# The opening stage of a decoder trunk: sums of squares, the first modulation columns and the rope angles computed on other engines

## The chip, the cores and the metric

The kernel runs on one core of one Trainium2 chip. The core has TensorE (PE: matmuls, with a separate record for each load of a stationary operand, PEld), VectorE (DVE), ScalarE (ACT), GpSimd (POOL) and SyncE (SP, which here only issues DMAs). The metric is the time of one execution on the device in microseconds (us), as the median of the runs shown.

## The reference

One layer of a decoder trunk over 512 tokens of 1024 features: a mixer of three branches (RWKV-7, forgetting attention, latent attention), then a squared-ReLU MLP, each behind a normalisation that is scaled and shifted by values computed from a vector `c`. The part that the change touches is this:

```python
c_act = jax.nn.silu(c)
mod = c_act @ w_mod[l] + b_mod[l]
sh_m, sc_m, g_m, sh_f, sc_f, g_f = [m[:, None, :] for m in jnp.split(mod, 6, axis=-1)]
h = rms_norm(x, norm_mix_pre[l]) * (1 + sc_m) + sh_m
z = h @ w_in[l]
```

and, for the rotary embedding of the latent attention:

```python
ang = positions.astype(jnp.float32)[..., None] * inv_freq
cos, sin = jnp.cos(ang), jnp.sin(ang)
```

`w_mod` is 1024 x 6144, `w_in` 1024 x 5572. Everything is float32; large products are made as three matmuls of a high and a low part (fp32r).

## The kernel before

x lies transposed: features on partitions, in 8 blocks of 128 features by 512 tokens. Scale and shift are then one number per partition: `A` and `B`, columns `d` of `self.mod[0]` and `self.mod[1]`. Block d of h is `x[d] * A * bc + B`, where `bc` holds each token's reciprocal root mean square on all partitions. `startup` (L370) does the following, in an order that is written by hand for TensorE, VectorE, ScalarE and GpSimd; SP's queue issues in program order too.

- **Loads.** `c` (one row), `cols` (small vectors as columns), the positions, four pieces of x on SP's queue, then for each block the two columns' weights `wm` (2 x 512 KB, three buffers) and the block's 896 columns of `w_in`, `raw` (448 KB, three buffers).
- **Warm-up.** `heat(n)` (L388) issues n matmuls of 128 columns on zeros, whose result isn't used. `WARM` gives the counts at five places.
- **Conditioning** (L200). `c` is broadcast to all partitions by a matmul with a row of ones, ScalarE takes tanh, VectorE forms `crow` = 2 silu(c) on all partitions, in two halves.
- **Sums of squares** (L398 to L414). ScalarE squares each block of x. VectorE adds five of them into `ssum[0]`, GpSimd three (blocks 2, 3, 4) into `ssum[1]`; TensorE sums over the partitions with 8 matmuls of one column. `rstd` and `spread` make a diagonal matrix of it, and a matmul with ones (L437) gives `bc`.
- **The block loop** (L440). For block d, `wm_load` issues the load of `wm` and computes the scale column: a product of 128 x 1024 with `crow` with its sum over the row (`mod_col`, L219), then `A` (L428). The shift column is made the same way on VectorE for block 0, and for the others by GpSimd (the product, L222) and ScalarE (the sum, L223, and the bias, L460). ScalarE rounds `raw` to `whi` (L454); VectorE makes `t` (L461), ScalarE `hi` (L462), VectorE `wlo` (L463) and `lo` (L464); then TensorE adds 21 matmuls of 512 columns to seven accumulators `zps` (L472).
- **Rope angles** (L266). A generator whose four parts are called in blocks 3 to 6 of that loop; the first three are VectorE's range reduction, the last two sines on ScalarE (with a load of their table).

Behind the loop `attn_inputs` (L479) reads `zps` and goes on with the rest of the mixer; only TensorE's order is by hand there.

Of the kernel before, what the change touches and what calls it, by code (L numbers as in the profile page):

```python
# [12 lines left out]
F32 = mybir.dt.float32  # L13
# [5 lines left out]
ALU = mybir.AluOpType  # L19
# [30 lines left out]
OUT_CUTS = (0, 384, 768, 1024)  # L50
LAST_CUTS = (0, 512, 768, 1024)
HC = 16
WARM = (1, 12, 0, 8, 4)
SUM_POOL = (2, 3, 4)
MOD0_DVE = (0,)
ROPE_D = (3, 4, 5, 6)
MM3 = 0.64
GATE_A = 7
FILL_G = 1.7
# [10 lines left out]
def _layout(fields):  # L70
# [11 lines left out]
    ("qg", 3), ("kvg", 2), ("bf", 4), ("cmul", 5), ("cadd", 5), ("invf", 32),  # L82
))
CST, NCST = _layout((
    ("bones", 128), ("dinc", 128), ("dexc", 128), ("cmask", 128),
# [13 lines left out]
class Builder:  # L99
# [99 lines left out]

    def conditioning(self, pool, pz, c):  # L200
        nc = self.nc
        th = pool.tile([P, D], F32, name="th")
        ps = [pz.tile([P, S], F32, tag="z", name="cps") for i in range(2)]
        for i in range(2):
            nc.tensor.matmul(ps[i], self.ones[0:1, :], c[:, i * S:(i + 1) * S], start=True, stop=True)
        for i in range(2):
            sl = slice(i * S, (i + 1) * S)
            nc.scalar.activation(th[:, sl], ps[i], AF.Tanh, scale=0.5)
            yield
            nc.vector.scalar_tensor_tensor(self.crow[:, sl], th[:, sl], 1.0, ps[i], ALU.add, ALU.mult)  # L210

    def pair(self, tag, name):
        return self.yp.tile([P, 2 * S], F32, tag=tag, name=name, bufs=3 if tag == "y" else 4)
# [3 lines left out]

    def mod_col(self, dst, w, cols=slice(0, D)):
        self.nc.vector.scalar_tensor_tensor(w, w, 0.5, self.crow[:, cols], ALU.mult, ALU.mult, accum_out=dst)  # L219

    def mod_col_pool(self, dst, w):
        self.nc.gpsimd.tensor_tensor(w, w, self.crow, ALU.mult)  # L222
        self.nc.scalar.activation(w, w, AF.Copy, scale=0.5, accum_out=dst)  # L223

    def mod_stream(self):
        for n, (i, d) in enumerate((i, d) for i in (2, 3, 4) for d in range(NB)):
# [143 lines left out]
    def startup(self, pz, pm):  # L370
        nc, tc, a = self.nc, self.tc, self.a
        E = mybir.EngineType
        with tc.tile_pool(name="sp", bufs=1, side="right") as sp, \
                tc.manual_schedule(engines={E.PE, E.DVE, E.Activation, E.Pool}):
            c = sp.tile([1, D], F32, name="c")
            nc.sync.dma_start(c, a["crow"])
            nc.scalar.dma_start(self.cols, a["cols"])
            self.pos = sp.tile([P, NT], I32, name="pos")
            nc.scalar.dma_start(self.pos, a["pos"])
            xt = [sp.tile([P, 2, S], F32, name=f"xt{i}") for i in range(4)]  # L380
            for i in range(4):
# [4 lines left out]
            nc.gpsimd.memset(warm, 0.0)  # L386

            def heat(n, ps=bc):  # L388
                for _ in range(n):
                    nc.tensor.matmul(ps[:, 0:P], self.ones, warm[:, 0:P], start=True, stop=True)  # L390

            heat(WARM[0])
            b1 = self.sml("b1", NB)
            rope = self.rope_tables(sp)
            cond = self.conditioning(sp, pz, c)
            next(cond, None)
            ssum = [sp.tile([P, S], F32, name=f"ssum{i}") for i in range(2)]
            for d in range(NB):  # L398
                own = d in SUM_POOL
                begin = d in (0, SUM_POOL[0])  # L400
                sq = ssum[own] if begin else sp.tile([P, S], F32, tag="sq", name="sq", bufs=4)
                nc.scalar.activation(sq, x[d], AF.Square)
                if d in (1, 3):
                    next(cond, None)
                if not begin:
                    (nc.gpsimd if own else nc.vector).tensor_tensor(ssum[own], ssum[own], sq, ALU.add)
            nc.vector.tensor_scalar(b1, self.col("b0", 0, NB), 1.0, None, ALU.add)
            heat(WARM[1])
            sums = pz.tile([P, S], F32, tag="z", name="sums")
            for i in (1, 0):  # L410
                for t in range(NT):
                    nc.tensor.matmul(sums[:, t:t + 1], ssum[i][:, t * P:(t + 1) * P], self.ones[:, 0:1],
                                     start=i == 1 and t == 0, stop=i == 0 and t == NT - 1)
                    heat(WARM[2])  # L414
            wms, accs = [], []

            def wm_load():
                d = len(wms)
                wm = sp.tile([P, 2, D], F32, tag="wm", name="wm", bufs=3)
                if d < 2:  # L420
                    nc.sync.dma_start(wm[:, 0, :], a["wmod"][:, d, 0, :])
                    nc.sync.dma_start(wm[:, 1, :], a["wmod"][:, d, 1, :])
                else:
                    nc.sync.dma_start(wm, a["wmod"][:, d, 0:2, :])
                acc = [self.sml(f"acc{i}") for i in range(2)]
                self.mod_col(acc[0], wm[:, 0, :])
                A = self.mod[0][:, d:d + 1]
                nc.vector.scalar_tensor_tensor(A, acc[0], b1[:, d:d + 1], self.col("gpre", d), ALU.add, ALU.mult)  # L428
                wms.append(wm)
                accs.append(acc)  # L430

            wm_load()
            rc = self.rstd(sums[:, 0:NT], 1.0 / D)
            diag = sp.tile([P, S], F32, name="diag")
            self.spread(diag, rc)
            heat(WARM[3])
            nc.tensor.matmul(bc, self.ones, diag, start=True, stop=True)  # L437
            self.h = ([], [])
            zps = [pz.tile([P, S], F32, tag="z", name=f"z{i}") for i in range(7)]
            for d in range(NB):  # L440
                if d:
                    wm_load()
                wm, acc = wms[d], accs[d]
                raw = self.rp.tile([P, 896], F32, tag="wr", name="wraw")
                nc.sync.dma_start(raw, a["wz0"][:, d, :])
                if d == 6:
                    nc.sync.dma_start(self.cstt, a["cst"])
                whi = self.wp.tile([P, 896], F32R, tag="wh", name="whi")
                wlo = self.wp.tile([P, 896], F32R, tag="wl", name="wlo")
                A, B = self.mod[0][:, d:d + 1], self.mod[1][:, d:d + 1]  # L450
                t = sp.tile([P, S], F32, tag="ht", name="ht", bufs=2)
                hi = self.hp.tile([P, S], F32R, tag="h", name=f"hh{d}")
                lo = self.hp.tile([P, S], F32R, tag="h", name=f"hl{d}")
                nc.scalar.activation(whi, raw, AF.Copy)  # L454
                if d in MOD0_DVE:
                    self.mod_col(acc[1], wm[:, 1, :])
                    nc.vector.tensor_tensor(B, acc[1], self.col("b1", d), ALU.add)
                else:
                    self.mod_col_pool(acc[1], wm[:, 1, :])
                    nc.scalar.activation(B, acc[1], AF.Identity, bias=self.col("b1", d))  # L460
                nc.vector.scalar_tensor_tensor(t, x[d], A, bc, ALU.mult, ALU.mult)  # L461
                nc.scalar.activation(hi, t, AF.Identity, bias=B)  # L462
                nc.vector.tensor_tensor(wlo, raw, whi.bitcast(F32), ALU.subtract)  # L463
                nc.vector.scalar_tensor_tensor(lo, t, B, hi.bitcast(F32), ALU.add, ALU.subtract)  # L464
                self.h[0].append(hi)
                self.h[1].append(lo)
                if d == 0:
                    heat(WARM[4], zps[6])
                first, last = d == 0, d == NB - 1
                for w, r in ((whi, hi), (wlo, hi), (whi, lo)):  # L470
                    for i in range(7):
                        nc.tensor.matmul(zps[i], w[:, i * P:(i + 1) * P], r, start=first and w is whi and r is hi,  # L472
                                         stop=last and r is lo)
# [1095 lines left out]
def layout(x, c, positions, w_in, mu_shift, w0, w_decay_up, a0, w_aaa_up, w_gate_up, k_k, k_a, r_k, ln_x_g, ln_x_b,  # L1569
# [18 lines left out]
        "bf": np.tile(arr(b_forget).reshape(1, 4), (P, 1)), "cmul": cmul, "cadd": cadd,  # L1588
        "invf": np.tile(np.float32(10000.0) ** (-np.arange(0, 64, 2, dtype=np.float32) / np.float32(64)), (P, 1)),
    }  # L1590
    for i, o in enumerate(order):
# [3 lines left out]
    ins["wmod"] = c_(wm.transpose(3, 2, 1, 0))  # L1595
    wi = arr(w_in)[0]

    def tb(w, cols_):
# [47 lines left out]
```

## Time and profile before

| | |
|---|---|
| median of 3 runs | 876.34 us (876.29 to 876.96) |
| the profiled execution | 875.69 us, span 873.9 us |
| mean granted clock of TensorE | 0.989 |
| z products of the opening stage | 168 matmuls, L472 |
| VectorE's column products in the first 70 us | 12, 1.22 us each where free |
| GpSimd's column products | 7, 2.40 us (median) |

How to read it: times are from the start of the span. The page gives busy time by engine and the chain of work that ended last, followed back from the last instruction. The timeline has one line for each instruction, or for several alike in a row: start, time, engine, line, operation, out<-in, shapes, count, and in brackets the idle time of the engine before it and what ended that. The windows view gives, for a stretch of time, its length, then busy time and number of instructions of PE, PEld, DVE, ACT and POOL, the granted clock (1.00 is full), the share of the DMA engines and the GB/s. An fp32 matmul leaves two records, an fp32r matmul one.

### The profile page before, as it was taken

Reading aid. Unit: us, or ns where it says so; the run is one execution under the profiler, and the core shown is the slowest. Engines: PE = TensorE matmul, PEld = TensorE weight load, DVE = VectorE, ACT = ScalarE, POOL = GpSimd, SP = SyncE. Lnnn points to the kernel's source line nnn. Section 1 sums busy time; section 2 is a strip of 40 time slices with the busy share of each in tenths; the row PEclk is TensorE's granted clock in tenths of the full one; section 3 lists DMA queues with packets and bytes.
Section 4 is the critical chain, followed back from the end, with each engine's and each line's share of the span. In section 5 each row is a group of like instructions: output and inputs, shape, how many; then the busy total and the mean of one; then the engine's idle time right before and its main releaser. Section 6 shows DMA issues by size and latency. Waiting matters only on the chain.

```text
span 873.9 us, 12074 instructions
## 1 busy us (share of the span) xinstructions
PE 845.9 (97%) x4520; PEld 699.8 (80%) x4520; DVE 524.8 (60%) x1053; ACT 381.5 (44%) x855; POOL 95.6 (11%) x129
## 2 busy tenths in 40 slices
PE   8889996999999999999999999999999999999997
PEld 6668786788877888886788889888888888888886
DVE  6998865887489755344586686442236543233465
ACT  5458663765462232424654775432314343122331
POOL 4410003000021089200000110000000000000000
PEclk9999997999999999999999999999999999999999
DMA  9764221111246732311136402432246432333311
GB/s 353 244 216 168 66 64 40 42 62 52 96 134 210 258 111 91 115 50 49 32 109 223 169 25 77 141 97 84 88 145 214 144 121 85 97 106 98 97 49 72
DMA packets 32635, 102.56 MB, mean 117 GB/s; under 512 B 5873, under 2 KB 7553, under 8 KB 31810
## 3 DMA queue, kind: packets, MB, share of 16 engines
q1 hardware_dynamic: 32002, 100.94, 34.9%
q0 software_dynamic: 288, 0.79, 0.3%
q8 instruction: 35, 0.57, 0.3%
q14 instruction: 22, 0.18, 0.1%
q10 hardware_dynamic: 288, 0.08, 0.0%
HBM read 99.16 MB, written 2.63 MB: 116 GB/s over the span
## 4 chain that ended last, share of the span: by engine, by line
PE 84%; DVE 9%; ACT 3%; issue 2%; DMA 1%; POOL 1%; SPq 0%; DVEq 0%; POOLq 0%; ACTq 0%
PE acc L148 24%; PE acc L150 23%; PE acc L149 23%; DVE wm L219 2%; DVE wlo L463 1%; PE z L472 1%; PE tp L717 1%; DMA xt<-xT 1%; DVE hl L464 1%; DVE mod L428 1%; PE pu L1027 1%; PE pr L1186 1%; DMA wm<-wmod 0%; PE py L1203 0%; PE pv L734 0%
## 5 line engine op out<-in xcount | busy, mean ns | idle before, releaser
L121 DVE TENSOR_TENSOR wlo<-wraw,whi 128x512 fp32r<-128x512 f32 (+4 forms) x260 | 165.6, 656 | 197.5 <-ACT whi L120 197.1
L120 ACT ACTIVATE whi<-wraw 128x512 fp32r<-128x512 f32 (+4 forms) x260 | 145.3, 587 | 295.1 <-PE acc L149 178.1
L148 PE MATMUL acc<-g,whi 128*128 128x512 f32 (+1 forms) x304 | 108.3, 356 | 0.0
L149 PE MATMUL acc<-g,whi 128*128 128x512 f32 (+1 forms) x304 | 108.1, 356 | 0.0
L150 PE MATMUL acc<-g,wlo 128*128 128x512 f32 (+1 forms) x304 | 108.1, 356 | 0.0
L148 PE MATMUL acc<-hh,whi 128*128 128x512 f32 x256 | 105.2, 411 | 0.0
L150 PE MATMUL acc<-hh,wlo 128*128 128x512 f32 x256 | 100.4, 392 | 0.6 <-DVE wlo L121 0.6
L149 PE MATMUL acc<-wlo,uh 128*128 128x512 f32 (+1 forms) x262 | 100.8, 385 | 0.0
L148 PE MATMUL acc<-whi,uh 128*128 128x512 f32 (+1 forms) x262 | 100.7, 384 | 0.0
L150 PE MATMUL acc<-whi,ul 128*128 128x512 f32 (+1 forms) x262 | 100.7, 384 | 0.0
L149 PE MATMUL acc<-hl,whi 128*128 128x512 f32 x256 | 100.1, 391 | 0.0
L219 DVE SCALAR_TENSOR_TENSOR wm<-wm,crow 128x1024 f32<-128x1024 f32 x41 | 52.2, 1274 | 24.1 <-DMA wm<-wmod 24.1
L148 PEld LDWEIGHTS acc<-g,whi 128*128 128x128 f32 x304 | 57.5, 189 | 8.2
L150 PEld LDWEIGHTS acc<-g,wlo 128*128 128x128 f32 x304 | 57.5, 189 | 8.1
L149 PEld LDWEIGHTS acc<-g,whi 128*128 128x128 f32 x304 | 57.5, 189 | 8.1
L150 PEld LDWEIGHTS acc<-hh,wlo 128*128 128x128 f32 x256 | 48.1, 188 | 11.7 <-DVE wlo L121 1.0
L149 PEld LDWEIGHTS acc<-wlo,uh 128*128 128x128 f32 x262 | 49.2, 188 | 10.1 <-DVE wlo L121 0.4
L150 PEld LDWEIGHTS acc<-whi,ul 128*128 128x128 f32 x262 | 49.2, 188 | 9.8
L148 PEld LDWEIGHTS acc<-whi,uh 128*128 128x128 f32 x262 | 49.2, 188 | 9.8
L148 PEld LDWEIGHTS acc<-hh,whi 128*128 128x128 f32 x256 | 48.5, 190 | 10.1 <-issue 0.2
L149 PEld LDWEIGHTS acc<-hl,whi 128*128 128x128 f32 x256 | 48.3, 189 | 8.1
L706 ACT ACTIVATE p<-sc,nb 128x128 f32<-128x128 f32 (+3 forms) x32 | 16.8, 526 | 28.3 <-DVE nb L704 14.7
(435 smaller groups left out, 1485.9 us busy)
## 6 DMA issues: line engine op xcount, KB each, us to landing
wm<-wmod SPq DMA_DIRECT2D x36, 512.0 KB, 4.3
wraw<-wu SPq DMA_DIRECT2D x32, 512.0 KB, 3.3
wraw<-wd SPq DMA_DIRECT2D x24, 512.0 KB, 3.3
wraw<-wgb SPq DMA_DIRECT2D x16, 512.0 KB, 3.4
wm<-wmod SPq DMA_DIRECT2D x6, 1024.0 KB, 6.8
wraw<-wz SPq DMA_DIRECT2D x10, 512.0 KB, 3.4
wraw<-wga SPq DMA_DIRECT2D x8, 512.0 KB, 3.6
wraw<-wo SPq DMA_DIRECT2D x8, 512.0 KB, 4.4
```

Of the source, the lines that this page charges most:

```text
L120: nc.scalar.activation(hi, src, AF.Copy)
L121: nc.vector.tensor_tensor(lo, src, hi.bitcast(F32), ALU.subtract)
L148: mm(out, lhs[0], rhs[0], start=start, stop=False)
L149: mm(out, lhs[0], rhs[1], start=False, stop=False)
L150: mm(out, lhs[1], rhs[0], start=False, stop=stop)
L219: self.nc.vector.scalar_tensor_tensor(w, w, 0.5, self.crow[:, cols], ALU.mult, ALU.mult, accum_out=dst)
L428: nc.vector.scalar_tensor_tensor(A, acc[0], b1[:, d:d + 1], self.col("gpre", d), ALU.add, ALU.mult)
L463: nc.vector.tensor_tensor(wlo, raw, whi.bitcast(F32), ALU.subtract)
L464: nc.vector.scalar_tensor_tensor(lo, t, B, hi.bitcast(F32), ALU.add, ALU.subtract)
L472: nc.tensor.matmul(zps[i], w[:, i * P:(i + 1) * P], r, start=first and w is whi and r is hi, stop=last and r is lo)
L706: nc.scalar.activation(p[:, 0:n], ps[:, 0:n], AF.Exp, bias=nb, scale=scale, accum_out=den)
L717: nc.tensor.transpose(tp[:, kb, :], p[:, kb * P:(kb + 1) * P], self.ident)
```

## The change

- `c` is activated before it is broadcast: ScalarE and VectorE work on one row of 1024 numbers, and TensorE broadcasts the result; ScalarE copies it to `crow`, the first half behind `bc`'s matmul, the second in block 0. `c` is also loaded as columns (8 per partition, `ccol`) and activated there.
- Sums of squares: for each block four matmuls of one column on the squares themselves, accumulated over the 8 blocks. No additions on VectorE or GpSimd.
- Scale and shift of blocks 0 and 1 (`PE_MODS`): 16 matmuls of one column each (`pe_mods`) from weights in another layout (`wmc`), block 0's between the sums and `bc`'s matmul, block 1's behind block 0's z products. Of blocks 2 to 7 both columns on VectorE. `mod_ends` makes A and B.
- `bc` is copied to SBUF (`bcs`), which blocks 1 to 7 read.
- Loads run two blocks ahead in program order; `wm` has four buffers. `cst` is loaded in block 4 in place of 6.
- The rope angles are computed while the squares are, the sines in block 3. A square root is taken ahead of the squares on a constant.
- Warm-ups: 12 ahead of the broadcast, 4 behind the sums, 4 behind block 0's columns, 2 before block 0's z products; before 1, 12, 8 and 4.

```diff
-WARM = (1, 12, 0, 8, 4)
-SUM_POOL = (2, 3, 4)
-MOD0_DVE = (0,)
-ROPE_D = (3, 4, 5, 6)
+WARM = (12, 4, 4, 0, 2)
+PE_MODS, WM_BUFS = 2, 4
+ROPE_S, ROPE_SIN = (0, 1, 2), 3
...
     def conditioning(self, pool, pz, c):
         nc = self.nc
-        th = pool.tile([P, D], F32, name="th")
+        th = pool.tile([1, D], F32, name="th")
+        nc.scalar.activation(th, c, AF.Tanh, scale=0.5)
+        nc.vector.scalar_tensor_tensor(c, th, 1.0, c, ALU.add, ALU.mult)
+        yield
         ps = [pz.tile([P, S], F32, tag="z", name="cps") for i in range(2)]
         for i in range(2):
-            nc.tensor.matmul(ps[i], self.ones[0:1, :], c[:, i * S:(i + 1) * S], start=True, stop=True)
-        for i in range(2):
             sl = slice(i * S, (i + 1) * S)
-            nc.scalar.activation(th[:, sl], ps[i], AF.Tanh, scale=0.5)
+            nc.tensor.matmul(ps[i], self.ones[0:1, :], c[:, sl], start=True, stop=True)
             yield
-            nc.vector.scalar_tensor_tensor(self.crow[:, sl], th[:, sl], 1.0, ps[i], ALU.add, ALU.mult)
+            nc.scalar.activation(self.crow[:, sl], ps[i], AF.Copy)
...
             heat(WARM[0])
+            ccol = self.col("c", 0, NB)
+            th = self.sml("thc", NB)
+            nc.scalar.activation(th, ccol, AF.Tanh, scale=0.5)
             b1 = self.sml("b1", NB)
+            nc.vector.tensor_scalar(b1, self.col("b0", 0, NB), 1.0, None, ALU.add)
+            nc.vector.tensor_scalar(th, th, 0.5, 0.5, ALU.mult, ALU.add)
+            nc.vector.tensor_tensor(ccol, ccol, th, ALU.mult)
             rope = self.rope_tables(sp)
             cond = self.conditioning(sp, pz, c)
-            next(cond, None)
+            next(cond)
+            nc.scalar.activation(self.sml("warmup"), self.eps, AF.Sqrt)
+            next(cond)
...
+            for d in range(PE_MODS):
+                for i in range(2):
+                    nc.sync.dma_start(wms[d][:, i], a["wmc"][:, d, i])
+                raw_load()
+            sums = pz.tile([P, S], F32, tag="z", name="sums")
             for d in range(NB):
...
-                if not begin:
-                    (nc.gpsimd if own else nc.vector).tensor_tensor(ssum[own], ssum[own], sq, ALU.add)
...
+                sq = sp.tile([P, S], F32, tag="sq", name="sq", bufs=4)
                 nc.scalar.activation(sq, x[d], AF.Square)
+                if d in ROPE_S:
+                    next(rope)
                 for t in range(NT):
+                    nc.tensor.matmul(sums[:, t:t + 1], sq[:, t * P:(t + 1) * P], self.ones[:, 0:1],
+                                     start=d == 0 and t == 0, stop=d == NB - 1 and t == NT - 1)
             rc = self.rstd(sums[:, 0:NT], 1.0 / D)
             diag = sp.tile([P, S], F32, name="diag")
             self.spread(diag, rc)
-            heat(WARM[3])
+
+            def pe_mods(d, ps):
+                for i in range(2):
+                    for k in range(NB):
+                        nc.tensor.matmul(ps[:, i:i + 1], wms[d][:, i, k * P:(k + 1) * P], ccol[:, k:k + 1],
+                                         start=i == 0 and k == 0, stop=i == 1 and k == NB - 1)
+                mod_ends(d, ps[:, 0:1], ps[:, 1:2])
+
+            def mod_ends(d, *acc):
+                A, B = self.mod[0][:, d:d + 1], self.mod[1][:, d:d + 1]
+                nc.vector.scalar_tensor_tensor(A, acc[0], b1[:, d:d + 1], self.col("gpre", d), ALU.add, ALU.mult)
+                nc.vector.tensor_tensor(B, acc[1], self.col("b1", d), ALU.add)
+
+            heat(WARM[1])
+            pe_mods(0, pz.tile([P, S], F32, tag="z", name="mods"))
+            heat(WARM[2])
             nc.tensor.matmul(bc, self.ones, diag, start=True, stop=True)
+            next(cond)
+            bcs = sp.tile([P, S], F32, name="bcs")
...
             for d in range(NB):
-                if d:
-                    wm_load()
...
+                if d + PE_MODS < NB:
+                    n = d + PE_MODS
+                    if n >= len(wms):
+                        wms.append(sp.tile([P, 2, D], F32, tag="wm", name="wm", bufs=WM_BUFS))
+                    nc.sync.dma_start(wms[n], a["wmod"][:, n, 0:2, :])
+                    raw_load()
...
+                if d >= PE_MODS:
+                    acc = [self.sml(f"acc{i}") for i in range(2)]
+                    for i in range(2):
+                        self.mod_col(acc[i], wms[d][:, i, :])
+                    mod_ends(d, *acc)
...
-                nc.vector.scalar_tensor_tensor(t, x[d], A, bc, ALU.mult, ALU.mult)
+                nc.vector.scalar_tensor_tensor(t, x[d], A, bcs if d else bc, ALU.mult, ALU.mult)
                 nc.scalar.activation(hi, t, AF.Identity, bias=B)
+                if d == 0:
+                    next(cond, None)
+                    nc.scalar.activation(bcs, bc, AF.Copy)
...
-                if d in ROPE_D:
+                if d + 1 < PE_MODS:
+                    pe_mods(d + 1, pm.tile([P, S], F32, tag="m", name="mods"))
+                if d == ROPE_SIN:
                     next(rope)
```

More of the change, by code (lines that the diff above doesn't have):

```diff
@@ L81 @@
     ("mu", 8), ("a0", 2), ("k_k", 2), ("k_a", 2), ("r_k", 2), ("ln_g", 2), ("ln_b", 2),
-    ("qg", 3), ("kvg", 2), ("bf", 4), ("cmul", 5), ("cadd", 5), ("invf", 32),
+    ("qg", 3), ("kvg", 2), ("bf", 4), ("cmul", 5), ("cadd", 5), ("invf", 32), ("c", 8),
 ))
@@ L219, in mod_col @@
         self.nc.vector.scalar_tensor_tensor(w, w, 0.5, self.crow[:, cols], ALU.mult, ALU.mult, accum_out=dst)
-    def mod_col_pool(self, dst, w):
-        self.nc.gpsimd.tensor_tensor(w, w, self.crow, ALU.mult)
-        self.nc.scalar.activation(w, w, AF.Copy, scale=0.5, accum_out=dst)
     def mod_stream(self):
@@ L397, in startup, with raw_load @@
-            ssum = [sp.tile([P, S], F32, name=f"ssum{i}") for i in range(2)]
+            next(cond)
+            nc.scalar.activation(self.sml("warmup"), self.eps, AF.Sqrt)
+            next(cond)
+            wms = []
+            for d in range(3):
+                wms.append(sp.tile([P, 2, D], F32, tag="wm", name="wm", bufs=WM_BUFS))
+            raws = []
+            def raw_load():
+                d = len(raws)
+                raws.append(self.rp.tile([P, 896], F32, tag="wr", name="wraw"))
+                nc.sync.dma_start(raws[d], a["wz0"][:, d, :])
@@ L398, in startup @@
+            for d in range(PE_MODS):
[3 more added lines that the diff above has]
+            sums = pz.tile([P, S], F32, tag="z", name="sums")
             for d in range(NB):
-                own = d in SUM_POOL
-                begin = d in (0, SUM_POOL[0])
-                sq = ssum[own] if begin else sp.tile([P, S], F32, tag="sq", name="sq", bufs=4)
+                sq = sp.tile([P, S], F32, tag="sq", name="sq", bufs=4)
@@ L402, in startup @@
                 nc.scalar.activation(sq, x[d], AF.Square)
-                if d in (1, 3):
-                    next(cond, None)
-                if not begin:
[L406 to L410, printed above, removed]
-                for t in range(NT):
-                    nc.tensor.matmul(sums[:, t:t + 1], ssum[i][:, t * P:(t + 1) * P], self.ones[:, 0:1],
-                                     start=i == 1 and t == 0, stop=i == 0 and t == NT - 1)
-                    heat(WARM[2])
@@ L415, in startup @@
[L415 to L430, printed above, removed]
@@ L440, in startup @@
             for d in range(NB):
-                if d:
[L442 to L446, printed above, removed]
+                if d + PE_MODS < NB:
+                    n = d + PE_MODS
+                    if n >= len(wms):
+                        wms.append(sp.tile([P, 2, D], F32, tag="wm", name="wm", bufs=WM_BUFS))
+                    nc.sync.dma_start(wms[n], a["wmod"][:, n, 0:2, :])
+                    raw_load()
+                raw = raws[d]
+                if d == 4:
                     nc.sync.dma_start(self.cstt, a["cst"])
@@ L454, in startup @@
                 nc.scalar.activation(whi, raw, AF.Copy)
[L455 to L461, printed above, removed]
+                nc.vector.scalar_tensor_tensor(t, x[d], A, bcs if d else bc, ALU.mult, ALU.mult)
                 nc.scalar.activation(hi, t, AF.Identity, bias=B)
+                if d == 0:
+                    next(cond, None)
+                    nc.scalar.activation(bcs, bc, AF.Copy)
                 nc.vector.tensor_tensor(wlo, raw, whi.bitcast(F32), ALU.subtract)
@@ L1590, in layout @@
     }
+    cols["c"] = tcol(c)
     for i, o in enumerate(order):
@@ L1595, in layout @@
     ins["wmod"] = c_(wm.transpose(3, 2, 1, 0))
+    ins["wmc"] = c_(wm[:, 0:2, 0:PE_MODS].reshape(NB, P, 2, PE_MODS, P).transpose(1, 3, 2, 0, 4).reshape(P, PE_MODS, 2, D))
     wi = arr(w_in)[0]
```

## The prediction

> **What bounds the kernel now.** I read the page first, then the chain of waits, then the timeline of the first 70 us, which is all that the change touches.
>
> ```profile
> span 873.9 us, 12074 instructions
> PE 845.9 (97%) x4520; PEld 699.8 (80%) x4520; DVE 524.8 (60%) x1053; ACT 381.5 (44%) x855; POOL 95.6 (11%) x129
> PE 84%; DVE 9%; ACT 3%; issue 2%; DMA 1%; POOL 1%; SPq 0%; DVEq 0%; POOLq 0%; ACTq 0%
> ```
>
> TensorE carries 84% of the chain that ended last, VectorE 9%. Behind the opening stage TensorE hardly stops, so I carry a shift of that stage's end through to the end of the kernel one for one. The TensorE timeline shows the stage (columns: start us, us, engine, line, operation, names, shapes, count, idle before):
>
> ```profile
> 1.46 0.80 PE L390 MATMUL bc<-warm,ones 128*128 128x128 f32 x2 [1.46 <-POOL warm L386]
> 2.49 3.78 PE L205 MATMUL cps<-c,ones 1*128 1x512 f32 x4 [0.23 <-DMA c<-crow]
> 6.19 5.20 PE L390 MATMUL bc<-warm,ones 128*128 128x128 f32 x24
> 11.37 1.05 PE L412 MATMUL sums<-ones,ssum 128*128 128x1 f32 x8
> 12.71 1.05 PE L412 MATMUL sums<-ones,ssum 128*128 128x1 f32 x8 [0.29 <-DVE ssum L406]
> 16.50 1.67 PE L437 MATMUL bc<-diag,ones 128*128 128x512 f32 x2
> 18.00 1.05 PE L390 MATMUL z<-warm,ones 128*128 128x128 f32 x8
> 19.93 1.89 PE L472 MATMUL z<-hh,whi 128*128 128x512 f32 x7 [0.87 <-ACT hh L462]
> ...
> 27.97 3.33 PE L472 MATMUL z<-hh,whi 128*128 128x512 f32 x7 [2.96 <-ACT hh L462]
> ...
> 34.45 1.75 PE L472 MATMUL z<-hh,whi 128*128 128x512 f32 x7
> 36.04 1.75 PE L472 MATMUL z<-hh,wlo 128*128 128x512 f32 x7
> ...
> 66.33 1.75 PE L472 MATMUL z<-hl,whi 128*128 128x512 f32 x7
> 67.92 0.31 PE L148 MATMUL n<-nh,hh 128*128 128x324 f32 x1
> ```
>
> The sums are done at 13.76, the z products run from 19.93 to 67.92: 48.0 us. Groups of seven follow each other by 1.59 us (34.45 to 36.04, 227 ns a matmul), so a block of 21 takes 4.77 us and eight take 38.2. About 10 us are lost to gaps, because h comes late. VectorE's own timeline says why (one GpSimd row among it):
>
> ```profile
> 26.35 0.75 DVE L461 SCALAR_TENSOR_TENSOR ht<-xt,mod,bc 128x512 f32<-128x512 f32 x1
> 27.02 1.08 DVE L463 TENSOR_TENSOR wlo<-wraw,whi 128x896 fp32r<-128x896 f32 x1
> ...
> 28.02 0.75 DVE L464 SCALAR_TENSOR_TENSOR hl<-ht,mod,hh 128x512 fp32r<-128x512 f32 x1
> ...
> 28.68 1.22 DVE L219 SCALAR_TENSOR_TENSOR wm<-wm,crow 128x1024 f32<-128x1024 f32 x1
> ...
> 29.82 0.09 DVE L219 DVE_READ_ACCUMULATOR wm<-wm,crow 128x1 f32 x1
> ...
> 29.95 0.22 DVE L428 SCALAR_TENSOR_TENSOR mod<-acc,b,cols 128x1 f32<-128x1 f32 x1
> ...
> 30.20 0.75 DVE L461 SCALAR_TENSOR_TENSOR ht<-xt,mod,bc 128x512 f32<-128x512 f32 x1
> 30.40 2.39 POOL L222 TENSOR_TENSOR wm<-wm,crow 128x1024 f32<-128x1024 f32 x1 [4.10 <-DMA wm<-wmod]
> ...
> 30.87 2.87 DVE L463 TENSOR_TENSOR wlo<-wraw,whi 128x896 fp32r<-128x896 f32 x1
> ```
>
> The same wlo subtraction takes 1.08 us alone and 2.87 beside GpSimd's product: 1.8 us lost. The groups of the first 70 us show it in the mean (1537 ns where a free one is 1080):
>
> ```profile
> L463 DVE TENSOR_TENSOR wlo<-wraw,whi 128x896 fp32r<-128x896 f32 x8 | 12.3, 1537 | 0.0
> ```
>
> **The change, part by part.**
>
> *GpSimd's products go; VectorE takes the shift columns of blocks 2 to 7.* Those stalls go (some 1.8 us a block), and one more column product comes. From start to start in the rows above, a block on VectorE is then: ht 0.67, wlo 1.00, hl 0.66, two column products 2 x 1.14, reading the accumulator 0.13, the scale A 0.25, the shift B between 0 and 0.22 (as A's row), taken as 0.15. Sum 5.14 us, above TensorE's 4.77, so VectorE sets the pace from block 2 on. ScalarE loses its two helpers per block (the copy with sum and B) and is not late.
>
> *Blocks 0 and 1: 16 one-column matmuls each on TensorE.* A one-column fp32 matmul leaves two records: 4 matmuls of the sums left 8 records in 1.05 us, about 113 ns from one to the next. So 32 records cost 3.6 us. VectorE stands idle for those of block 1: its A and B wait for them, and ht, wlo and hl of block 1 and all of block 2 are queued behind A. TensorE's own queue puts them behind block 0's z products.
>
> *Sums of squares on TensorE.* 8 x 4 matmuls, 64 records, in place of 16: 7.2 us at 113 ns, with nothing left to VectorE and GpSimd. The squares still come at the pace of x:
>
> ```profile
> 9.98 1.15 ACT L402 ACTIVATE sq<-xt 128x512 f32<-128x512 f32 x2 [0.53 <-DMA xt<-xT]
> 11.15 1.28 ACT L161 ACT_TABLE_LOAD   x1
> 16.10 2.35 POOL L222 TENSOR_TENSOR wm<-wm,crow 128x1024 f32<-128x1024 f32 x1 [4.79 <-DMA wm<-wmod]
> 18.39 0.74 DVE L461 SCALAR_TENSOR_TENSOR ht<-xt,mod,bc 128x512 f32<-128x512 f32 x1
> 19.16 0.72 ACT L462 ACTIVATE hh<-ht,mod 128x512 fp32r<-128x512 f32 x1 [4.25 <-DVE ht L461]
> ```
>
> The last square ends at 11.1, so the sums can't end before 12.1; with TensorE free from about 6.4 they end at 13.7 at best, as now. Then, in TensorE's order, come 4 warm-up matmuls, block 0's 16 columns, 4 warm-ups and only then bc, which now starts right behind the diagonal. That is new work on the path that sets the end.
>
> *The clock under that work.* The windows view, cut at the times where the granted clock changes (3.41 us apart, also at 133.84), gives busy time, instructions, and the clock after PEclk's place (the third number from the end):
>
> ```profile
> 10.97:14.38 3.41, 3.12 (x27) 2.87 (x26) 3.17 (x7) 2.03 (x4) 0.34 (x1) 1.00 1.03 421
> 14.38:17.80 3.42, 3.42 (x14) 2.80 (x13) 3.38 (x4) 0.53 (x1) 1.70 (x1) 0.50 1.04 432
> 45.10:48.52 3.42, 1.73 (x8) 1.43 (x9) 3.35 (x7) 2.51 (x4) 0.00 (x0) 1.00 0.77 266
> 130.43:133.84 3.41, 1.16 (x10) 0.95 (x9) 2.17 (x5) 1.72 (x4) 3.18 (x8) 1.00 0.20 28
> 137.25:140.67 3.42, 2.17 (x11) 2.20 (x12) 2.49 (x7) 1.76 (x4) 1.70 (x4) 0.50 0.00 0
> ```
>
> A window 51% busy with wide matmuls keeps the full clock, one 34% busy loses it. The first window is 91% busy but 2.1 us of it are the one-column sums, 1.1 us wide warm-ups: it loses the clock as a 34% window would. One-column matmuls hardly count. The sums and columns of the change are 64 + 32 such records in a row, so they run mostly at half clock. Price of one there: no such row exists. From above, warm-ups at half clock come 217 ns apart (24 in 5.20); from below, 113. The nearest rows are 128-column matmuls whose weight load is the longer part:
>
> ```profile
> 139.28 0.42 PE L760 MATMUL sc<-fkb,fqb 128*128 128x128 f32 x1
> 139.49 0.41 PE L761 MATMUL sc<-cmaskr,identr 128*128 128x128 f32 x1
> ...
> 144.54 0.22 PE L761 MATMUL sc<-cmaskr,identr 128*128 128x128 f32 x1
> 144.60 0.60 PE L799 MATMUL pk<-ident,kr 128*64 128x128 f32 x4
> ```
>
> 210 ns apart at half clock, 60 at full: the load slows with the clock. I take 217 and keep 113 for the range.
>
> The Trainium skill, "TensorE: Matmul & The Clock Gate", section "LDWEIGHTS (loading the stationary operand)", gives a weight load as its columns divided by 1.2, in ns, with no clock in it. By it a one-column record would stay near 107 ns and the change would cost what the first rival says; the 210 ns spacing speaks against it.
>
> *Start and rope.* The warm-ups before c grow from 1 to 12 (24 records at 217 ns: 1.46 to 6.7; less where the clock rises on the way), and cover the activation of c, two instructions of 1024 elements on one row, about 1.2 us each by L219's row. The table load of 1.28 us at 11.15 moves ahead of the squares, and the rope angles move from blocks 3 to 6 to where VectorE has no sums to add any more: I cost both at nothing, the cover being the wait for x (the last squares now wait for it). If that cover were gone, 1.3 us. On SP's queue the loads keep their order, two blocks ahead, with four wm buffers; a block's 128 x (2 x 1024 + 896) x 4 bytes = 1.51 MB at 421 GB/s (first of the windows above) take 3.6 us, less than 5.14, and block 1's wm is there by 16.1. No wait of a load reaches TensorE.
>
> **The sum.** The warm-ups bring the full clock at the window end near 4.1 (14.38 - 3 x 3.41; they fill 78% of that window, and 63% did not do it at 140.67, so this is open). They end at 5.5, c's broadcast (two of the four records of 3.78 us, at full clock half of 1.9) at 6.4, the sums start at 6.5. Up to 10.97, 39 records at 113 ns; 25 more at 217: end 16.3. Then warm-ups 8 x 0.217 = 1.7, columns 32 x 0.217 = 6.9, warm-ups 1.7, bc 1.7 and 0.2 to wake VectorE, ht 0.77, hh 0.77 (18.39, 19.16, 19.93): z starts at 30.0. Now it is 19.93.
> From there: block 0, 4.8; block 1's columns 3.6 (full clock by then) and 0.1 to wake VectorE: A of block 1 at z + 8.5. VectorE: A and B 0.4, ht, wlo, hl 2.3, block 2's columns, A and B 2.8, ht and hh 1.5: block 2's products at z + 15.6; five more blocks at 5.14: block 7 at z + 41.3; its products 4.8: end at z + 46.1. That is 2 us shorter than the 48.0 of now, and ends at 76.1 in place of 67.92: **8.2 us later**. The profiled execution took 875.69 us (span 873.9, the rest around it); its median runs lie 0.65 above it. 876.34 + 8.2 = **884.5 us**.
>
> **Rivals.**
> 1. *The load does not slow with the clock.* Records at 113 ns: sums end at 13.7 to 15.6, columns 3.6, z starts at 24 to 26, its end 70 to 74 with some z groups at half clock: 878.2 to 882. For it: nothing but the missing row; against it, the 210 ns.
> 2. *The warm-ups never bring the full clock, or lose it at 7.6.* Sums end at 19 to 22, z starts at 33 to 36, and z's first groups run at 427 ns: end 80 to 86, that is 888.5 to 894. For it: the 63% window; against: 12 warm-ups in one piece.
> 3. *The other side: the clock holds through the sums and columns.* Then sums 13.7, columns 17.3 plus warm-ups, bc at 20.2, z at 21.8, end at 67.9: no change. If in addition VectorE's block falls below TensorE's 4.77 (B hidden, column products overlapping their accumulator reads), z from block 1 on runs without gaps: 21.8 + 8.5 + 1.9 + 7 x 4.77 = 65.6, or 874.0. It decides at 4.77 us a block. Against it: the window 10.97 to 14.38.
> 4. *The stalls are not GpSimd's.* Then they stay, 10 us on top. Each long row of VectorE lies beside a GpSimd row; I give it little.
>
> **Chances.** Forecast (882 to 888.5) 0.42; rival 1 0.20; rivals 2 and 4 0.13; rival 3 with no change 0.11, with the gain 0.14. A measurement here tells 0.2%, 1.8 us, from no change. Faster 0.14, same 0.11, slower 0.75. The range must leave out no more than 0.2: 873.8 (rival 3's gain) to 890 (into rival 2).
>
> **What would show it.** Right: sums' records 217 ns apart behind 11 us and a clock of 0.5 there; z starting near 30; a gap of about 5.5 us in z between blocks 0 and 1; VectorE without rows above 1.3 us; blocks about 5.1 us apart from 2 to 7. Wrong: a full clock through the sums, z starting before 24, or blocks at 4.8.

## The result, and the profile after

| | before | after |
|---|---|---|
| median of 4 runs each, on one chip | 876.32 us | 889.0 us (888.68 to 890.3) |
| ratio | | 1.015, 95% interval 1.0133 to 1.0168 |
| profiled execution, span | 873.9 us | 887.2 us |
| mean granted clock | 0.989 | 0.976 |
| first z product, end of z | 19.93, 67.92 us | 33.60, 80.06 us |

The change makes the kernel 12.7 us slower; 884.5 us, 8.2 slower, was forecast. The page after, its lines on the span, the engines and the chain of work that ended last:

```profile
span 887.2 us, 12250 instructions
PE 864.8 (97%) x4626; PEld 720.6 (81%) x4626; DVE 510.5 (58%) x1063; ACT 374.5 (42%) x838; POOL 74.6 (8%) x120
PE 89%; DVE 7%; ACT 1%; issue 1%; POOL 1%; DVEq 0%; POOLq 0%; ACTq 0%
PE acc L147 24%; PE acc L149 23%; PE acc L148 23%; PE z L484 4%; PE sums L422 1%; PE mods L431 1%; PE tp L731 1%; PE bc L386 1%; DVE wlo L120 1%; PE pr L1200 1%; PE pv L748 1%; PE py L1217 0%; PE pu L1041 0%; PE pas L1142 0%; PE xtp L1395 0
```

TensorE's part of the chain grew from 84% to 89%, VectorE's fell from 9% to 7%. That is no gain: the sums (L422), the columns (L431) and the warm-ups (L386) now stand on the chain with about 1% each. TensorE's timeline after, in the stretch that was shown of before:

```profile
1.46 4.68 PE L386 MATMUL bc<-warm,ones 128*128 128x128 f32 x24 [1.46 <-POOL warm L382]
6.07 1.12 PE L208 MATMUL cps<-c,ones 1*128 1x512 f32 x2
7.12 12.54 PE L422 MATMUL sums<-ones,sq 128*128 128x1 f32 x64
19.53 2.05 PE L386 MATMUL bc<-warm,ones 128*128 128x128 f32 x8
21.38 6.83 PE L431 MATMUL mods<-cols,wm 128*128 128x1 f32 x32
...
29.91 1.91 PE L443 MATMUL bc<-diag,ones 128*128 128x512 f32 x2
...
33.60 1.87 PE L484 MATMUL z<-hh,whi 128*128 128x512 f32 x7
...
38.50 3.63 PE L431 MATMUL mods<-cols,wm 128*128 128x1 f32 x32
44.05 3.35 PE L484 MATMUL z<-hh,whi 128*128 128x512 f32 x7 [1.92 <-ACT hh L471]
47.20 2.85 PE L484 MATMUL z<-hh,wlo 128*128 128x512 f32 x7
...
51.50 1.75 PE L484 MATMUL z<-hh,whi 128*128 128x512 f32 x7
...
56.26 1.75 PE L484 MATMUL z<-hh,whi 128*128 128x512 f32 x7
...
80.06 0.31 PE L147 MATMUL n<-nh,hh 128*128 128x324 f32 x1
```

Read it from the top. The 64 records of the sums take 12.5 us and end at 19.6 in place of 13.8. Block 0's 32 records take 6.83 us, 213 ns each, and the same 32 for block 1 take 3.63 us, 113 ns each. The first z product starts 13.7 us later than before. The z stage itself is 46.5 us against 48.0. Block 1's products wait until 44.05 and run at half speed (7 matmuls in 3.35 us; 1.75 in block 2), and from block 2 on the blocks follow each other by 4.76 us.

The windows view of TensorE alone, cut where the clock changes (busy time and number of records, granted clock, DMA share, GB/s):

```profile
1.46:5.14 3.68, 3.68 (x17) 1.00 0.81 241
5.14:8.55 3.41, 3.41 (x24) 1.00 1.03 407
8.55:11.97 3.42, 3.42 (x18) 0.50 1.01 409
...
32.40:35.86 3.46, 3.46 (x16) 0.99 0.34 79
39.27:42.68 3.41, 2.86 (x26) 1.00 0.00 0
42.68:46.09 3.41, 2.04 (x5) 0.50 0.24 34
```

In the first row the clock column says 1.00, but 17 warm-up records take 3.68 us, 216 ns each: half speed. The column can't be trusted ahead of its first change; the spacing of the records can. The full clock came at about 5.14, lasted one window of 3.41 us, and went at 8.55, 1.4 us into the sums. It came back only at 32.4, was gone again at 42.68 after a window of one-column work and idling, and so block 1's products lost time too.

VectorE's timeline over one block after, and the group of the wlo subtractions in the first 85 us (1537 ns in the mean before):

```profile
47.36 0.75 DVE L470 SCALAR_TENSOR_TENSOR ht<-xt,mod,bcs 128x512 f32<-128x512 f32 x1
48.03 1.08 DVE L475 TENSOR_TENSOR wlo<-wraw,whi 128x896 fp32r<-128x896 f32 x1
49.03 0.74 DVE L476 SCALAR_TENSOR_TENSOR hl<-ht,mod,hh 128x512 fp32r<-128x512 f32 x1
49.69 1.22 DVE L219 SCALAR_TENSOR_TENSOR wm<-wm,crow 128x1024 f32<-128x1024 f32 x1
...
51.99 0.08 DVE L219 DVE_READ_ACCUMULATOR wm<-wm,crow 128x1 f32 x1
51.99 0.21 DVE L437 SCALAR_TENSOR_TENSOR mod<-acc,b,cols 128x1 f32<-128x1 f32 x1
52.12 0.15 DVE L438 TENSOR_TENSOR mod<-acc,cols 128x1 f32<-128x1 f32 x1
52.23 0.75 DVE L470 SCALAR_TENSOR_TENSOR ht<-xt,mod,bcs 128x512 f32<-128x512 f32 x1
```

```profile
L475 DVE TENSOR_TENSOR wlo<-wraw,whi 128x896 fp32r<-128x896 f32 x8 | 8.7, 1084 | 0.0
```

The stalls beside GpSimd are gone, and a block costs VectorE 52.23 - 47.36 = 4.87 us.

Behind the opening the two traces keep their distance except in one place. The z stage ends 12.14 us later than before and the span 13.3 us later; most of the difference is this row of TensorE's timeline after, a wait that the kernel before doesn't have:

```profile
114.69 0.47 PE L147 MATMUL acc<-hh,whi 128*128 128x512 f32 x1 [1.33 <-DVE cum L646]
```

### The profile page after: what moved, and what is told of

It reads as the page before. It is cut to its first block, busy times and chain, and to the rows that moved or that the text cites. A ratio compares the mean times of both kernels' runs of the same rounds, so it can differ in the third digit from the quotient of the medians.

```text
span 887.2 us, 12250 instructions
## 1 busy us (share of the span) xinstructions
PE 864.8 (97%) x4626; PEld 720.6 (81%) x4626; DVE 510.5 (58%) x1063; ACT 374.5 (42%) x838; POOL 74.6 (8%) x120
## 4 chain that ended last, share of the span: by engine, by line
PE 89%; DVE 7%; ACT 1%; issue 1%; POOL 1%; DVEq 0%; POOLq 0%; ACTq 0%
PE acc L147 24%; PE acc L149 23%; PE acc L148 23%; PE z L484 4%; PE sums L422 1%; PE mods L431 1%; PE tp L731 1%; PE bc L386 1%; DVE wlo L120 1%; PE pr L1200 1%; PE pv L748 1%; PE py L1217 0%; PE pu L1041 0%; PE pas L1142 0%; PE xtp L1395 0%
```

## The experiments

Theory: the loss is one-column work on TensorE, dear because it doesn't hold the clock, and block 1's columns standing in the z stage; the end of GpSimd's products is a real gain that this buries. Rivals: warm-ups or loads are late, the early rope costs, or the gain isn't GpSimd's. Edits are against the changed kernel where nothing else is said; medians are of runs beside the kernel before on the same chip. That kernel's own median was 876.32 us beside the changed kernel, 875.51 beside e1 to e4, 874.94 beside e5 to e8 and 875.32 beside e9 to e11, so medians of different groups compare to about 1 us; across groups the ratios are the safer numbers.

| run | median | ratio to before, 95% | first z | end of z |
|---|---|---|---|---|
| e1: sums and columns 128 wide | 880.54 | 1.0048 (1.0029 to 1.0067) | 22.72 | 72.91 |
| e2: all columns on VectorE | 875.62 | 0.9998 (0.9988 to 1.0008) | 28.15 | 67.27 |
| e3: sums as before | 886.9 | 1.0115 (1.0091 to 1.0139) | 31.04 | 78.24 |
| e4: both | 869.37 | 0.9927 (0.9905 to 0.995) | 20.95 | 60.14 |
| e5: e2, sums 512 wide | 875.95 | 1.0006 (0.9993 to 1.002) | 23.65 | 64.90 |
| e6: no middle warm-ups | 887.65 | 1.014 (1.0117 to 1.0162) | 31.21 | 78.55 |
| e7: e4 and GpSimd products | 884.54 (2 runs) | 1.0103 (1.0075 to 1.0131) | 20.97 | 73.13 |
| e8: e5 and one PSUM tile | 880.4 (one run) | | 23.45 | 64.78 |
| e9: e4, sums mixed | 868.75 | 0.9924 (0.9906 to 0.9942) | 20.51 | 59.69 |
| e10: e9, fewer warm-ups | 869.99 | 0.9942 (0.9926 to 0.9959) | 21.94 | 62.54 |
| e11: the changed kernel again | 888.35 (one run) | | 33.16 | 79.28 |

### e1: the same matmuls, 128 columns wide

```diff
-                    nc.tensor.matmul(sums[:, t:t + 1], sq[:, t * P:(t + 1) * P], self.ones[:, 0:1],
+                    nc.tensor.matmul(sums[:, t * P:(t + 1) * P], sq[:, t * P:(t + 1) * P], self.ones,
...
-                        nc.tensor.matmul(ps[:, i:i + 1], wms[d][:, i, k * P:(k + 1) * P], ccol[:, k:k + 1],
+                        nc.tensor.matmul(ps[:, i * P:(i + 1) * P], wms[d][:, i, k * P:(k + 1) * P], ccol[:, k:k + 1].broadcast_to([P, P]),
```

> The change, with the same 48 matmuls for sums and for block 0's and 1's columns (weight loads, count, order), but 128 columns wide in place of one; only the first column of each result is read. Theory (one-column matmuls do not count as activity, so the clock falls to half and each record takes 213 ns): wide ones hold the clock, records come 114 ns apart, the sums end near 14.5 in place of 19.6, block 0's columns take 3.6 us in place of 6.8, z starts near 23 in place of 33.6, and the kernel takes 877 to 880 us. Rival (a record costs 213 ns there for another reason, such as reading squares or weights just written): wider matmuls can only be as slow or slower, 889 us or more.

TensorE's timeline of e1:

```profile
7.49 7.41 PE L422 MATMUL sums<-ones,sq 128*128 128x128 f32 x64
...
15.63 3.74 PE L431 MATMUL mods<-cols,wm 128*128 128x128 f32 x32
...
22.72 1.89 PE L484 MATMUL z<-hh,whi 128*128 128x512 f32 x7
...
44.16 1.86 PE L484 MATMUL z<-hh,whi 128*128 128x512 f32 x7
...
50.10 1.88 PE L484 MATMUL z<-hh,whi 128*128 128x512 f32 x7 [0.91 <-ACT hh L471]
```

The same products, with 128 times as many columns of result, are faster: 116 ns a record throughout, and no change of the clock is recorded in the first 72 us. The z stage starts 10.9 us earlier than in the changed kernel. So the clock is the cost, and width pays for it. In total some 8 us come back (880.54 us, just above the 877 to 880 expected), less than z's start gains: VectorE now takes a third column product, one of those for the later parts of the layer, in most blocks, which then follow by 5.94 us (44.16 to 50.10).

### e2, e3 and e4: each part put back, and both

e2 makes all columns on VectorE and copies `crow` while the squares are made; e3 adds the squares on VectorE and GpSimd as before; e4 does both. Early rope, early activation of c and no GpSimd products stay in all three.

```diff
-PE_MODS, WM_BUFS = 2, 4
+PE_MODS, AHEAD, WM_BUFS = 0, 2, 4
...
-            pe_mods(0, pz.tile([P, S], F32, tag="z", name="mods"))
```

```diff
+            ssum = [sp.tile([P, S], F32, name=f"ssum{i}") for i in range(2)]
...
+                if not begin:
+                    (nc.gpsimd if own else nc.vector).tensor_tensor(ssum[own], ssum[own], sq, ALU.add)
+            heat(12)
+            for i in (1, 0):
...
+                    nc.tensor.matmul(sums[:, t:t + 1], ssum[i][:, t * P:(t + 1) * P], self.ones[:, 0:1],
+                                      start=i == 1 and t == 0, stop=i == 0 and t == NT - 1)
```

> The change with PE_MODS = 0: the scale and shift columns of blocks 0 and 1 on VectorE as well, none on TensorE; the sums of squares stay on TensorE. Both halves of crow are copied during the squares. Theory: block 0's columns (2.3 us) lie beside the sums, which end near 20; the 6.8 us before bc and the gap of 7 us between z's blocks 0 and 1 go, blocks come 4.9 us apart: z starts near 27, ends near 67 to 68: 876 to 878 us. Rival (VectorE becomes the bound of the start, because block 0's and 1's four columns delay its ht): z ends above 72, 881 us or more.

> The change with the sums of squares as they were before (five blocks added on VectorE, three on GpSimd, 8 one-column matmuls, 12 warm-ups ahead of them); columns of blocks 0 and 1 stay on TensorE. Theory: the sums end near 14 in place of 19.6 and all behind them moves with it, part of block 0's columns at full clock: 880 to 884 us. Rival (the sums' time is hidden behind the loads of x and wm): 888 to 889 us.

> Both undone: sums of squares as before, all columns of all eight blocks on VectorE, so that of the change there stay the removal of GpSimd's products, the early rope angles and the activation of c ahead of its broadcast. Theory (GpSimd's products stalled VectorE by some 1.8 us a block, and only TensorE's one-column work gave that back): z starts at 18 to 20, blocks 4.9 to 5.1 us apart, ends at 58 to 61: 866 to 870 us, faster than the kernel before. Rival (VectorE with 16 columns is as late as with GpSimd's stalls): 875 to 878 us.

TensorE's timeline of e3:

```profile
14.21 1.87 PE L429 MATMUL sums<-ones,ssum 128*128 128x1 f32 x8 [1.81 <-DVE ssum L425]
15.94 2.05 PE L386 MATMUL bc<-warm,ones 128*128 128x128 f32 x8
17.79 6.83 PE L438 MATMUL mods<-cols,wm 128*128 128x1 f32 x32
```

and of e4:

```profile
6.19 1.98 PE L208 MATMUL cps<-c,ones 1*128 1x512 f32 x4
8.10 4.58 PE L386 MATMUL bc<-warm,ones 128*128 128x128 f32 x24
...
13.90 1.05 PE L431 MATMUL sums<-ones,ssum 128*128 128x1 f32 x8 [0.43 <-DVE ssum L427]
...
20.95 1.89 PE L490 MATMUL z<-hh,whi 128*128 128x512 f32 x7 [1.15 <-ACT hh L478]
...
25.91 1.89 PE L490 MATMUL z<-hh,whi 128*128 128x512 f32 x7
...
60.14 0.31 PE L147 MATMUL n<-nh,hh 128*128 128x324 f32 x1
```

The four kernels make a square; the corner with both parts, the changed kernel, ran on another chip than the other three. Columns on TensorE cost 889.0 - 875.62 = 13.4 us with the new sums and 886.9 - 869.37 = 17.5 with the old ones. The new sums cost 6.25 us without the columns. With the columns there the difference is 2.1 us, and the intervals of the two ratios (1.015 and 1.0115) overlap, so it is not clear of noise. In total e4 came as expected and e2 0.4 us below its range; both start z about 1 us later than expected. e3 missed (880 to 884). Its sums end at 16.1 and not near 14, because TensorE waits 1.81 us for VectorE's last addition. Of the 3.6 us that it still gains at the sums' end, 2.6 reach the first z product, and its columns, at half clock, still take 6.83 us.

e4 beats both kernels. Its z stage takes 39.2 us, 8.8 less than before; that is the change's gain, but not that of GpSimd's products alone. The rope angles left the stage too: before, their rows on VectorE filled 3.1 us of it (40.26 to 41.45, 47.50 to 48.03 and 53.71 to 55.08). No run puts them back alone, so up to some 3 of the 8.8 us, an estimate from these rows, may be theirs. e4's blocks are 4.9 us apart, VectorE's pace.

The first two rows of e4 say more of the clock. The granted clock reads 1.00 up to 8.80 and 0.50 from there to 12.2. The window of 3.41 us that ends at 8.80 is busy throughout: about 1.5 us of it (44%) are 128-column warm-ups, and 1.9 us are the broadcast of `c`, matmuls of 512 columns that use one of the 128 rows. In e7 the clock falls at 10.13 behind a window of the same make-up. If the broadcast counted as the warm-ups do, these windows would be full. So it isn't only one-column work that fails to hold the clock.

### e7: GpSimd beside VectorE again

e4 with two products per block on GpSimd, which nothing reads, behind `hi` of blocks 1 to 7:

```diff
+                for i in range(2 if d else 0):
+                    nc.gpsimd.tensor_tensor(junk[:, i * S:(i + 1) * S], hi.bitcast(F32), self.crow[:, i * S:(i + 1) * S], ALU.mult)
```

> e4 with GpSimd work put back that nobody reads: behind hh of blocks 1 to 7 two products of 128 x 512 from SBUF into an unused tile, on GpSimd alone; VectorE's instructions and their order are those of e4. Theory (VectorE is stalled by GpSimd's products themselves): rows of VectorE beside them become 1 to 2 us longer, blocks come 6 to 7 us apart, 876 to 885 us. Rival (the stalls of before came from the waits and the order around GpSimd's products, not from the products): rows and blocks as in e4, 869 to 870 us.

VectorE's timeline of e7, and the GpSimd row beside it:

```profile
33.04 1.83 DVE L485 SCALAR_TENSOR_TENSOR hl<-ht,mod,hh 128x512 fp32r<-128x512 f32 x1
34.79 2.30 DVE L219 SCALAR_TENSOR_TENSOR wm<-wm,crow 128x1024 f32<-128x1024 f32 x1
```

```profile
33.02 2.98 POOL L481 TENSOR_TENSOR junk<-hh,crow 128x512 f32<-128x512 f32 x2 [4.06 <-ACT hh L479]
```

As the theory had it, VectorE's rows grow: the two VectorE instructions that fall beside the two products take 1.09 and 1.08 us longer than elsewhere; the third of the block, and wlo before them, don't. The z stage grows from 39.2 to 52.2 us, and the median is 15.2 us above e4's. The stalls were GpSimd's.

### e6 and e11: warm-ups, and the changed kernel again

e6 has `WARM = (12, 0, 0, 0, 2)` in place of `(12, 4, 4, 0, 2)`; e11 has no edit.

> The change without the two groups of 4 warm-ups around block 0's columns (WARM = 12, 0, 0, 0, 2). Theory (at half clock they only fill TensorE's queue ahead of bc, 1.7 to 1.85 us each): z starts 3.5 us earlier, 885 to 886 us, less some of it if z's first groups then run at half clock (up to 2 us). Rival (they bring the clock back for bc and z): no gain or a loss, 889 to 892 us.

> The changed kernel a second time, nothing edited, for one more profile. The clock fell at 8.8 us in the first profile, where the forecast had 10.97 from the windows of the kernel before. If the moment belongs to the execution and not to the program: another moment this time, anywhere in a window of 3.4 us, the end of the sums moving against it by about 1 us for each us (213 ns for 113 a record), and all that is behind moving with it. If it belongs to the program: the fall at 8.8 us and the sums' end at 19.6 us again, within 0.2. The wait of 1.33 us of the matmul on line 147 for cum near 114 us: if it is due to the program (buffer hand-out), there again; if to chance, gone, with the total about 1 us less.

e6 starts z at 31.21 in place of 33.60, but there the full clock comes back at 33.8 in place of 32.4, and z's first group takes 3.07 us in place of 1.87. z ends at 78.55, against 80.06 and 79.28 in the two profiles of the changed kernel. In the total no gain is clear of noise: the ratios to the kernel before are 1.014 and 1.015, with overlapping intervals. So the eight warm-ups take 3.7 us and give most of it back through the clock, and 887.65 us lies between the theory and the rival. TensorE's windows in e11:

```profile
3.93:7.34 3.41, 3.41 (x16) 1.00 1.03 384
7.34:10.70 3.36, 3.36 (x25) 1.00 1.00 383
10.75:14.16 3.41, 3.41 (x19) 0.50 1.02 418
```

16 records in the first row is half speed again, so here the full clock came at 7.34 and went at 10.75, 2.2 us later than in the first profile (8.55 by the cut above; 8.8 in the expectation was a coarser reading). The moment belongs to the execution. But the sums ended at 19.6 in both, since the rise comes later with the fall: the warm-ups then take 5.49 us in place of 4.68, and the sums start 1.0 us later. So that part of the expectation fell. The wait for cum is there again, 1.33 us: it belongs to the program.

### e5 and e8: sums without a diagonal, and another PSUM tile

e5 is e2 with `bc` made directly by wide matmuls, and a square root and a reciprocal of 128 x 512 numbers; e8 adds one unused PSUM tile to it.

```diff
+                nc.tensor.matmul(bc, self.ones, sq, start=d == 0, stop=d == NB - 1)
+            bcs = sp.tile([P, S], F32, name="bcs")
+            nc.scalar.activation(bcs, bc, AF.Sqrt, bias=self.eps, scale=1.0 / D)
+            nc.vector.reciprocal(bcs, bcs)
```

```diff
+            heat(1, pz.tile([P, S], F32, tag="z", name="hot"))
```

> All columns on VectorE as in e2, and the sums of squares on TensorE the other way round: the matrix of ones is the stationary operand and a block's squares are 512 moving columns (one matmul a block, 0.86 us at full clock, in place of four of one column); it leaves the sum on all partitions, so that a square root and a reciprocal of 128 x 512 give bc without the diagonal matrix and its matmul. Theory (TensorE is a good place for the sums as long as its matmuls are wide): the clock holds, the sums end near 12.5, bc is there near 14, block 0's columns set z's start at 17 to 19, blocks 4.9 us apart, z ends at 56 to 58: 864 to 867 us, faster than e4. Rival (a reciprocal of 512 elements a partition, or VectorE's order, costs what the diagonal did): 868 to 870 us.

> e5 with one more warm-up on a PSUM tile of its own, so that the banks of that pool are handed out one place further. Theory (TensorE's wait of 1.33 us for VectorE's second cum subtraction, some 34 us behind the z products, comes from the bank that the first accumulator behind the opening stage takes over): the wait goes and the kernel is 1.0 to 1.5 us faster than e5. Rival (the wait comes from VectorE being later there): it stays, time as e5's plus 0.2 us.

VectorE's timeline of e5:

```profile
16.34 3.35 DVE L425 RECIPROCAL bcs<-bcs 128x512 f32<-128x512 f32 x1 [7.40 <-ACT bcs L424]
```

e5 missed by some 10 us. The clock holds through the wide sums, as meant, but they end at 15.4 and not near 12.5: 16 records at 0.43 us are 6.9 us from their start at 7.2, and half of c's broadcast stands between them. Then the reciprocal takes 3.35 us, 6.5 ns a number in each partition, and block 0's columns are queued behind it. TensorE then waits 4.05 us for block 0, and block 0's products run at half clock. In e8, TensorE's timeline:

```profile
102.31 0.79 PE L147 MATMUL acc<-hh,whi 128*128 128x512 f32 x1 [4.19 <-DVE zr L886]
```

The wait for cum is gone and a longer one has come at the same place, on the same line. So how PSUM is handed out does change what this matmul waits for, in one run, but neither expectation holds. e1 has neither wait, and all others but e8 have the one for cum; which choice of the program brings it stays open.

### e9 and e10: a shorter path to the sums

e9 is e4 with VectorE alone adding blocks 0 to 5, 6 and 7 summed directly by TensorE, and block 0's columns ahead of the reciprocal. e10 is e9 with 2 warm-ups for 4 in two places, behind the sums and ahead of block 0's z products; the 8 ahead of the sums, which its expectation names, stay.

```diff
-WARM = (12, 4, 4, 0, 2)
+WARM = (12, 4, 0, 0, 4)
...
+                if 0 < d < 6:
+                    nc.vector.tensor_tensor(ssum, ssum, sq, ALU.add)
+                if d >= 6:
+                    sqs.append(sq)
+            heat(8)
+            for i, s in enumerate(sqs + [ssum]):
```

> Sums as before only for the squares of blocks 0 to 5, added by VectorE alone; the squares of blocks 6 and 7 go to TensorE directly, so 12 one-column matmuls in all and no addition on GpSimd. All columns on VectorE, block 0's ahead of the reciprocal of the root; 4 warm-ups behind the sums. Compared with the kernel with both parts put back (e4: first z at 20.95, blocks 4.88 apart, z end 60.1, 869.4 us). Theory (the opening's end is set by when the last squares are summed, and the blocks behind it by VectorE's 4.88 us): first z at 17 to 18.5, z end 56 to 58, total 865.5 to 868 us. Rival (block 0's columns now stand in front of the reciprocal on VectorE, or the clock falls in front of the sums, and the start is no earlier): first z at 20 to 21, 869 to 870 us.

> The kernel of e9 with 2 warm-ups rather than 4 ahead of the squares' sums' first group and 2 rather than 4 behind them. If warm-ups only fill time that TensorE waits anyway, same as e9 within 0.5 us. If they stand in the way (as the middle ones of the changed kernel did: 1.4 us for 8), up to 1 us less than e9. If they hold the clock, 1 to 2 us more, with the clock at half in the first z block.

TensorE's timeline of e9:

```profile
13.73 1.56 PE L432 MATMUL sums<-ones,ssum 128*128 128x1 f32 x8
15.15 2.05 PE L386 MATMUL bc<-warm,ones 128*128 128x128 f32 x8
17.00 1.91 PE L459 MATMUL bc<-diag,ones 128*128 128x512 f32 x2
...
20.51 2.05 PE L495 MATMUL z<-hh,whi 128*128 128x512 f32 x7
```

The additions end earlier (12.4 in place of 13.84), yet z starts at 20.5: the rival's start, with a total of 868.75 us just below its 869. The clock fell at 14.05, after which warm-ups and bc take twice their time (8 warm-up records 2.05 us, bc 1.91). e9's interval overlaps e4's. e10's median is 1.2 us above e9's, with overlapping intervals, and with the full clock from 27.0 in place of 20.9 and block 0's first group at 3.36 us. That fits warm-ups that hold the clock, but by e11 the moment also moves by 2 us from one execution to the next, so one profile each doesn't prove it.

## Why the prediction was right or wrong

**Where it is decided: right.** The loss arises in the opening and is carried to the end: 12.14 us at the end of z, 13.3 at the end of the span.

**GpSimd's products: right.** No VectorE row of a block is above 1.22 us after, and e7 brings the stalls back. They were sized as 1.8 us a block; e7's two products cost 2.2.

**VectorE's block: oversized.** 5.14 us was forecast, 4.87 measured, because the accumulator's read takes no time of its own (A starts with it at 51.99, 0.13 was counted) and A and B take 0.24 us together in place of 0.40. It didn't pace the changed kernel either. While block 1's products run at half clock, VectorE gets ahead, and TensorE sets 4.76 us from block 2 on. It does pace e4. From block 2 to block 7 that is 5 x (4.76 - 5.14) = -1.9 us, and block 1 at half clock, which wasn't counted, made good for it: block 2 starts 17.9 us behind block 0 (51.50 - 33.60) in place of 15.6. So the z stage of 46.1 us, measured 46.5, came out nearly right from two wrong terms. The gap of 5.5 us between blocks 0 and 1 was right (38.50 to 44.05).

**Columns, 3.6 us at full and 6.9 at half clock: right** (3.63 and 6.83).

**The price of a one-column record at half clock: right.** 217 ns was taken, 213 measured, and 113 at full clock. The Trainium skill, "TensorE: Matmul & The Clock Gate", section "LDWEIGHTS (loading the stationary operand)", has no clock in its figure, by which 128 columns come to an estimated 107 ns. The rows differ from it by twice at half clock, and the measurement decides: rival 1 is out. Of the rows by which the prediction chose 217, one was misread: its 60 ns at full clock (144.54 to 144.60) is the step to a matmul of another shape. The weight loads themselves, in the trace before, start 0.11 us apart at full clock (144.20, 144.31) and 0.22 at half (139.17, 139.39); that doubling is what the choice needed.

**The clock under the sums: the failed step.** "Up to 10.97, 39 records at 113 ns; 25 more at 217: end 16.3." The mechanism was right, one-column work loses the clock, but not the stretch at full speed. The step took it as 4.1 to 10.97, two windows, with the boundaries of the execution before, and gave no row for the second window. Measured is one window, 5.14 to 8.55: some 13 records at 113 ns and 51 at 213, 12.3 us, against 12.4 from the sums' start to the next row (7.12 to 19.53). The sums ended 3.2 us later than forecast, 0.6 of it because they started at 7.12 and not at 6.5; that is nearly all of the 3.6 us by which z started late. A second window would have needed more wide work in the window in which the sums began; the warm-ups reach 1.0 us into that window in the first profile (to 6.14) and not at all in e11. On the forecast's own times they reach 1.4 us into it (4.1 to 5.5), 41%, between its 34% that lost the clock and its 51% that kept it, with c's broadcast behind them; e4's window of 44% and a broadcast lost it. So the step would probably have failed on its own boundaries too. What came is rival 2's second branch, losing the clock at 7.6: its times (sums 19 to 22, z from 33, 888.5 to 894 us) are those measured, but block 0's z products ran at full clock and not at 427 ns each. The forecast's 882 to 888.5 us missed the 889.0; that the whole range up to 890 holds it is owed to the stretch of rival 2 that it takes in, not to the sum. The Trainium skill, same page, section "What's actually happening", says that the window runs freely and doesn't reset when a kernel starts. The two profiles of one program, 8.55 and 10.75, agree. A boundary read off one execution was no ground for the next.

**Rope, table and loads at nothing: right for the changed kernel**, where no PE wait in the opening is theirs. The cover named was that VectorE has no squares to add. With the additions back in e4, VectorE's last addition ends at 13.84 in place of 12.66, and the rope's rows stand between the additions. z starts there at 20.95, not at the old 19.93. That the rope is the cause was not tried alone.

**Nothing lost downstream: wrong by 1.3 us**, the wait for cum.

The sum of the errors: 3.6 (start) + 0.4 (z stage) + 1.2 (behind it) = 5.2 us, which with 8.2 makes the 13.3 us between the spans, rounding apart.

## What to carry to other kernels

Moving small reductions to an idle TensorE is not free where they stand on the path: ask what they do to its clock, and if they must be there, make them wide, as 128 columns took less time here than one (7.41 us for 12.54). Take out of a change what gains, and try it alone: removing GpSimd's work beside VectorE, together with moving the rope angles, was worth 8.8 us of the z stage and had been buried under columns that cost 13 to 17. For a free-running window, price the best and the worst alignment, never the one in the trace at hand.

## What the runs showed of the hardware

- 64 one-column records took 12.54 us, the same with 128 columns 7.41 us (e1).
- A fully busy window of 3.41 us, 1.5 us of it 128-column matmuls and 1.9 us matmuls of 512 columns that use one row, was followed by half clock (e4, at 8.80; e7, at 10.13).
- The clock column reads 1.00 ahead of its first recorded change, while records are spaced as at half clock (216 ns a warm-up record until 5.14 in the changed kernel).
- A reciprocal of 128 x 512 took 3.35 us on VectorE, where a product of 128 x 1024 with its sum takes 1.22.
- Each GpSimd product of 128 x 512 beside VectorE added 1.1 us to one VectorE instruction, whichever it was (0.74 to 1.83, 1.22 to 2.30).
